# Last expert of a mixture-of-experts block: three whole-row loads and one in two column halves, with tokens added in PSUM

## The chip, the cores and the metric

The kernel runs on one core of a Trainium2 chip. Times are microseconds of device time of one execution. Three executions of the kernel before gave a median of 1518.48 us, from 1516.9 to 1519.0. The profile shown is of a further execution, which took 1518.31 us itself, with a span of 1516.6 us between its first and last recorded instruction.

## The reference, cut to what matters

Two transformer blocks on 256 tokens of width 1024. The second ends in a mixture of 16 experts; each expert takes the 32 tokens that score highest for it, and the rows that it gives are added to the tokens. A final RMS norm closes the program. What runs ahead (first block, mixers, cross attention) is left out here.

```python
def ec_moe(h, router_w, w_gu, w_down):
    ...
    gates, idx = lax.top_k(jnp.swapaxes(aff, 1, 2), cap)          # cap = 32
    def expert(args):
        xe, wgu, wd = args
        gu = jnp.einsum('bcd,df->bcf', xe, wgu)                   # 1024 -> 4096
        ga, up = jnp.split(gu, 2, axis=-1)
        return jnp.einsum('bcf,fd->bcd', jax.nn.silu(ga) * up, wd)  # 2048 -> 1024
    ...                                                           # gate, scatter-add

x = x + ec_moe(rmsnorm_2(x, norm_ffn_g), router_w, w_gu, w_down)
return rmsnorm_2(x, final_norm_g)        # x * rsqrt(mean(x*x) + eps) * g
```

All is float32. One expert has 16 MB of gate and up weights and 8 MB of down weights.

## The kernel before, in words

The last part of the program is `moe`. For each expert `e` it loads the gate and up weights (`w_gu`, four loads of 4 MB from expert 2 on, 32 KB in a row on each partition) and the down weights (`w_down`, four loads of 2 MB, 16 KB in a row on each partition). All loads are issued by SyncE (SP) into a ring of slots, and a load waits until TensorE has read what its slot held. TensorE multiplies the 32 tokens with the gate and up weights as they land (L1314), ScalarE and VectorE make `silu(gate) * up` (L1334, L1335), TensorE turns that round (L1338), ScalarE copies it out (`aT`, L1340), and the helper `down(j, raw, c0, n)` multiplies it with row block `j` of the down weights into the PSUM tile `y[c0]` (L1347). The four row blocks of one expert are called loads 0 to 3 below. The helper `scatter(c0, n, out, ...)` copies `y[c0]` to SBUF (`ys`, by ScalarE at L1357 or VectorE at L1359) and multiplies it with the gated one-hot matrix `ogT` (L1361), which adds the expert's rows to the tokens, one matrix product for each of the two token tiles `t`. Experts 0 to 14 add up in four PSUM banks `acc[2 * t + n]` (token tile `t`, column half `n`).

After expert 14 VectorE adds the four banks to the tokens `x` (L1374). Expert 15 goes another way. Its loads 0 and 1 are whole-row loads (L1395). Load 2 comes in two column halves. Load 3 comes in columns 0 to 511, 512 to 767, 768 to 895 and 896 to 1023 (all at L1401). For each of these four column pieces (`cuts`) the kernel finishes the products, scatters them to fresh PSUM tiles, adds them to `x` (L1410) and takes the sum of squares (L1411). Then `rstd` makes 1/sqrt with a bit trick and three Newton steps on VectorE (L171 to L181), two operations scale the halves of each token tile (L1417 on ScalarE, L1418 on VectorE), and two stores of 512 KB end the program (L1420).

`rstd_q`, used in the first block, makes 1/sqrt from ScalarE's square root, a reciprocal and one Newton step (L257 to L268). The order of instructions on each engine comes from a scheduler; the context manager `strict` (L102) makes PE, VectorE and ScalarE keep the written order inside it.

## Time and profile before

| | |
|---|---|
| three executions | 1516.9 to 1519.0 us, median 1518.48 |
| the profiled execution | 1518.31 us, of which span 1516.6 us |
| TensorE / VectorE / ScalarE busy | 77% / 28% / 23% of the span |
| bytes read from HBM | 500.79 MB |
| expert part | from about 640 us to the end |
| last expert's down loads | 8 MB, then the scatter, the norm and two stores |

TensorE is busy the most, but in the expert part most of its idle time is spent waiting for weights. The page's 40 slices show how much the DMA engines moved in each fortieth of the span. The timeline has one line for a run of equal instructions, with start and length, and in brackets how long the engine had been idle and what ended that.

### The profile page before, as it was taken

Reading aid. Unit: us, or ns where it says so; the run is one execution under the profiler, and the core shown is the slowest. Engines: PE = TensorE matmul, PEld = TensorE weight load, DVE = VectorE, ACT = ScalarE, POOL = GpSimd, SP = SyncE. Lnnn points to the kernel's source line nnn. Section 1 sums busy time; section 2 is a strip of 40 time slices with the busy share of each in tenths; the row PEclk is TensorE's granted clock in tenths of the full one; section 3 lists DMA queues with packets and bytes.
Section 4 is the critical chain, followed back from the end, with each engine's and each line's share of the span. In section 5 each row is a group of like instructions: output and inputs, shape, how many; then the busy total and the mean of one; then the engine's idle time right before and its main releaser. Section 6 shows DMA issues by size and latency. Waiting matters only on the chain.

```text
span 1516.6 us, 17752 instructions
## 1 busy us (share of the span) xinstructions
PE 1162.6 (77%) x7704; PEld 690.8 (46%) x7704; DVE 424.4 (28%) x801; ACT 355.5 (23%) x614; POOL 7.0 (0%) x19
## 2 busy tenths in 40 slices
PE   7999999999999999885665656665656656556665
PEld 5989989999988776321121111121111112111112
DVE  6744567445568864200000000000000000000002
ACT  6545546434456733000000000000000000000002
POOL 1000000000000000000000000000000000000000
PEclk9999999999999999997888877889888889888788
DMA  9754538555643279999999999999999999999996
GB/s 304 226 167 139 167 116 273 182 184 191 201 131 99 85 293 423 393 430 428 433 431 425 432 425 434 429 427 433 429 428 431 430 427 434 430 426 432 427 431 239
DMA packets 98189, 502.98 MB, mean 332 GB/s; under 512 B 8107, under 2 KB 62143, under 8 KB 80960
## 3 DMA queue, kind: packets, MB, share of 16 engines
q1 hardware_dynamic: 98112, 501.85, 82.6%
q8 instruction: 60, 0.98, 0.3%
q14 instruction: 17, 0.14, 0.0%
HBM read 500.79 MB, written 1.05 MB: 331 GB/s over the span
## 4 chain that ended last, share of the span: by engine, by line
PE 70%; another core or an unknown queue 16%; DMA 5%; DVE 3%; SPq 2%; ACT 2%; issue 1%; DVEq 0%; ACTq 0%
PE acc L127 21%; PE sm L1314 18%; PE sm L127 10%; PE sm L1347 9%; PE acc L1361 4%; DMA eraw<-in_expert_w_down_dram 2%; DMA eraw<-in_expert_w_gu_dram 2%; SPq L1401 2%; PE sm L1284 1%; PE acc L1171 1%; PE sm L1338 1%; DVE es L1335 1%; DVE ys L1359 1%; ACT aT L1340 1%
## 5 line engine op out<-in xcount | busy, mean ns | idle before, releaser
L1314 PE MATMUL sm<-eraw,xs 128*32 128x512 f32 x2048 | 319.0, 779 | 222.9 <-DMA eraw<-in_expert_w_gu_dram 222.9
L1314 PEld LDWEIGHTS sm<-eraw,xs 128*32 128x32 f32 x2048 | 77.0, 138 | 447.4 <-issue 230.8
L74 DVE TENSOR_TENSOR whl<-raw,whl 128x1024 fp32r<-128x1024 f32 x152 | 181.7, 1221 | 105.9 <-ACT whl L73 104.8
L1347 PE MATMUL sm<-eraw,aT 128*32 128x512 f32 (+2 forms) x1088 | 145.1, 669 | 66.2 <-DMA eraw<-in_expert_w_down_dram 54.5
L73 ACT ACTIVATE whl<-raw 128x1024 fp32r<-128x1024 f32 x152 | 154.0, 1052 | 78.0 <-issue 47.2
L1335 DVE SCALAR_TENSOR_TENSOR es<-sm,rsl,es 128x512 f32<-128x512 f32 x16 | 12.0, 751 | 439.5 <-PE sm L1314 436.6
L1334 ACT ACTIVATE es<-sm,rsl 128x512 f32<-128x512 f32 x16 | 11.0, 687 | 408.4 <-PE sm L1314 408.4
L1347 PEld LDWEIGHTS sm<-eraw,aT 128*32 128x32 f32 x1088 | 32.5, 120 | 161.5 <-DMA eraw<-in_expert_w_down_dram 89.6
L127 PE MATMUL acc<-xh,whl 128*128 128x256 f32 x704 | 96.2, 285 | 0.0
L127 PE MATMUL sm<-xh,whl 128*128 128x256 f32 x704 | 91.4, 283 | 0.0
L127 PEld LDWEIGHTS acc<-xh,whl 128*128 128x128 f32 x704 | 88.4, 189 | 1.1
L127 PEld LDWEIGHTS sm<-xh,whl 128*128 128x128 f32 x704 | 87.9, 189 | 0.6
L1361 PE MATMUL acc<-ys,ogT 128*128 128x512 f32 (+2 forms) x136 | 65.2, 603 | 15.2 <-DVE ys L1359 14.4
L1359 DVE COPY ys<-sm 128x512 f32<-128x512 f32 (+2 forms) x18 | 11.4, 631 | 196.9 <-PE acc L1361 196.9
L127 PE MATMUL acc<-whl,xh 128*128 128x512 f32 x240 | 65.9, 405 | 0.2
L1332 ACT ACTIVATE ogT<-sm 128x256 f32<-128x256 f32 x16 | 6.1, 383 | 220.6 <-PE sm L1330 220.6
L127 PE MATMUL acc<-whl,aH 128*128 128x512 f32 x176 | 55.9, 390 | 0.0
L1357 ACT ACTIVATE ys<-sm 128x512 f32<-128x512 f32 x16 | 9.6, 597 | 196.5 <-PE sm L1347 196.5
L1361 PEld LDWEIGHTS acc<-ys,ogT 128*128 128x128 f32 x136 | 23.2, 193 | 59.8 <-DVE ys L1359 27.7
L127 PE MATMUL acc<-xl,whl 128*128 128x256 f32 x352 | 50.1, 283 | 0.0
L127 PEld LDWEIGHTS acc<-whl,xh 128*128 128x128 f32 x240 | 44.6, 190 | 10.9 <-ACT xh L162 0.8
L127 PE MATMUL sm<-xl,whl 128*128 128x256 f32 x352 | 49.4, 283 | 0.0
(392 smaller groups left out, 1171.6 us busy)
## 6 DMA issues: line engine op xcount, KB each, us to landing
eraw<-in_expert_w_gu_dram SPq DMA_DIRECT2D x56, 4096.0 KB, 53.0
eraw<-in_expert_w_down_dram SPq DMA_DIRECT2D x62, 2048.0 KB, 55.2
raw<-in_w_in_dram SPq DMA_DIRECT2D x34, 1024.0 KB, 5.4
eraw<-in_expert_w_gu_dram SPq DMA_DIRECT2D x16, 2048.0 KB, 16.1
raw<-in_w_gate_dram SPq DMA_DIRECT2D x11, 1024.0 KB, 5.3
raw<-in_w_up_dram SPq DMA_DIRECT2D x11, 1024.0 KB, 5.6
raw<-in_w_down_dram SPq DMA_DIRECT2D x11, 1024.0 KB, 5.0
raw<-in_w_out_dram SPq DMA_DIRECT2D x8, 1024.0 KB, 5.1
```

Of the source, the lines that this page charges most:

```text
L73: nc.scalar.activation(H[:, k], raw[:, k], AF.Copy)
L74: self.at["L"] = nc.vector.tensor_tensor(L[:, k], raw[:, k], H[:, k].bitcast(F32), OP.subtract).ins
L127: nc.tensor.matmul(out, l[i], r[j], start=first and p == 0 and q == 0, stop=last and p == 2 and q == n - 1)
L1171: nc.tensor.matmul(acc[c], o[:, k, t * 128:(t + 1) * 128], w[c][:, k, :], start=k == 0, stop=k == 3)
L1284: nc.tensor.matmul(pg[kk][:, i * 128:(i + 1) * 128], x[:, t, feats(k)], OH[:, t, e:e + 4, :].rearrange("p e s -> p (e s)"), start=t == 0, ...
L1314: nc.tensor.matmul(dst[32 * j:32 * j + 32, :], xs[:, k, 32 * q:32 * q + 32], raw[:, o + 512 * j:o + 512 * j + 512], start=k == 0, stop=k = ...
L1335: nc.vector.scalar_tensor_tensor(s, U, rs, s, OP.mult, OP.mult)
L1338: nc.tensor.transpose(p[:, c * 128:(c + 1) * 128], s[:, c:512:4], self.ident)
L1347: nc.tensor.matmul(y[c0][32 * c:32 * c + 32, 0:n], aT[:, c, 32 * j:32 * j + 32], raw[:, o:o + n], start=j == 0, stop=j == 3, tile_position ...
L1359: nc.vector.tensor_copy(ys, y[c0][:, 0:n])
L1361: nc.tensor.matmul(out[t], ogT[:, t * 128:(t + 1) * 128], ys, start=first, stop=last)
L1401: nc.sync.dma_start(raws[j].rearrange("p (i n) -> p i n", i=4)[:, :, c0:c0 + m], rows(j)[:, :, c0:c0 + m])
```

## The change

- The last expert's loads 0, 1 and 2 are whole-row loads now, and load 3 comes in two column halves, each with rows of 2 KB.
- The tokens `x` are added in PSUM: after expert 3's scatter, four products of `x` with the identity matrix go into `acc`. The VectorE additions at L1374 and L1410 are gone, and the last expert scatters into `acc` as all others do.
- The squares and the product with the gain read `acc` directly. The last two lines of each token tile scale what is in `fo`.
- The second half's `ys` is copied by VectorE (256 columns) and ScalarE (256 columns).
- `strict` fixes the order from load 3 to the stores. `rstd_q` takes both token tiles and replaces `rstd`; a small square root behind the last `silu` has ScalarE load the square root's table there.

```diff
-    def rstd_q(self, ss):
+    def rstd_q(self, *sums):
...
+        for ss in sums:
+            q = self.small.tile([128, 8], F32, name="rstq", tag="rsq", bufs=4)
+            v, d, h, y, t = (q[:, i:i + 1] for i in range(5))
+            nc.vector.tensor_scalar(v, ss[:, 0:1], ss[:, 1:2], 1.0 / D, OP.add, OP.mult)
+            nc.scalar.activation(d, v, AF.Sqrt, bias=self.eps)
+            nc.vector.tensor_scalar(h, v, -0.5, -0.5 * EPS, OP.mult, OP.add)
+            qs.append((d, h, y, t))
+        for d, h, y, t in qs:
+            nc.vector.reciprocal(y, d)
+            nc.vector.tensor_scalar(t, y, y, h, OP.mult, OP.mult)
+            nc.vector.tensor_scalar(y, t, 1.5, y, OP.add, OP.mult)
+        return y if len(sums) == 1 else [q[2] for q in qs]
...
                     ys = ew.tile([128, n], F32, name="ys", tag="ys")
-                    if c0 == 0:
+                    if e == NE - 1 and c0:
+                        nc.vector.tensor_copy(ys[:, 0:256], y[c0][:, 0:256])
+                        nc.scalar.activation(ys[:, 256:512], y[c0][:, 256:512], AF.Copy)
+                    elif c0 == 0:
...
+                if e == 3:
+
+                    for t in range(2):
+                        for n in range(2):
+                            nc.tensor.matmul(acc[2 * t + n], self.ident, x[:, t, 512 * n:512 * n + 512],
+                                             start=False, stop=False)
+
...
-            raws, y[768], y[896] = {}, self.ps(), self.ps()
-            cuts = ((0, 512), (512, 256), (768, 128), (896, 128))
-            for i, (c0, n) in enumerate(cuts):
...
+            with self.queued([silu]):
+                nc.scalar.activation(fo[:, 0, 0:1], self.eps, AF.Sqrt)
+            raws = [slot() for _ in range(4)]
+            for j in range(3):
+                nc.sync.dma_start(raws[j], rows(j).rearrange("p i n -> p (i n)"))
+                for n in range(2):
+                    down(j, raws[j], 512 * n, 512)
+            for n in range(2):
+                c = slice(512 * n, 512 * n + 512)
+                nc.sync.dma_start(raws[3].rearrange("p (i n) -> p i n", i=4)[:, :, c], rows(3)[:, :, c])
+            ss = [self.small.tile([128, 16], F32, name="ss", tag="st1", bufs=4) for _ in range(2)]
+            with self.strict():
+                for n in range(2):
+                    c = slice(512 * n, 512 * n + 512)
+                    down(3, raws[3], 512 * n, 512)
+                    scatter(512 * n, 512, acc[n::2], False)
+                    for t in range(2):
+                        nc.scalar.activation(junk, acc[2 * t + n], AF.Square, accum_out=ss[t][:, n:n + 1])
+                        nc.vector.tensor_tensor(fo[:, t, c], acc[2 * t + n], g[:, c], OP.mult)
+                r = self.rstd_q(*ss)
                 for t in range(2):
...
+                    nc.scalar.activation(fo[:, t, 0:512], fo[:, t, 0:512], AF.Copy, scale=r[t])
+                    nc.vector.tensor_scalar(fo[:, t, 512:D], fo[:, t, 512:D], r[t], None, OP.mult)
```

The loads of the last expert, as they stand on SyncE in the kernel before (`raw` slots of SBUF are called `eraw`; a wait on DMAHW waits for an earlier load, a wait on PE, DVE or Activation for that engine):

```order
L1377 DMA eraw<-in_final_norm_g_dram 1x1024 [waits DMAHW5_49,DMAHW1_49,PE_49]
L1395 DMA eraw<-in_expert_w_down_dram 128x4096 [waits DMAHW2_49]
L1395 DMA eraw<-in_expert_w_down_dram 128x4096 [waits DMAHW3_49]
L1401 DMA eraw<-in_expert_w_down_dram 128x4x512 [waits DMAHW4_49]
L1401 DMA eraw<-in_expert_w_down_dram 128x4x512
L1401 DMA eraw<-in_expert_w_down_dram 128x4x512 [waits DMAHW6_49]
L1401 DMA eraw<-in_expert_w_down_dram 128x4x256 [waits DMAHW7_49]
L1401 DMA eraw<-in_expert_w_down_dram 128x4x128 [waits DMAHW0_49]
L1401 DMA eraw<-in_expert_w_down_dram 128x4x128 [waits DMAHW1_49]
```

The same place in the changed kernel:

```order
L1386 DMA eraw<-in_final_norm_g_dram 1x1024 [waits DMAHW5_49,DMAHW1_49,PE_49]
L1396 DMA eraw<-in_expert_w_down_dram 128x4096 [waits DMAHW2_49]
L1396 DMA eraw<-in_expert_w_down_dram 128x4096 [waits DMAHW3_49]
L1396 DMA eraw<-in_expert_w_down_dram 128x4096 [waits DMAHW4_49]
L1401 DMA eraw<-in_expert_w_down_dram 128x4x512
L1401 DMA eraw<-in_expert_w_down_dram 128x4x512 [waits DMAHW6_49]
```

Eight down loads have become five, and the first half of load 3 stands behind three whole loads, where it stood behind two whole loads and a half.

VectorE from the last expert's first scatter result to the start of 1/sqrt, in the kernel before:

```order
L1410 TENSOR_TENSOR x<-x,acc 128x512 [waits PE_49]
L1413 TENSOR_TENSOR eraw<-x,eraw 128x512 [waits DMAHW2_49,DMAHW5_49,DMAHW1_49,DMAHW6_49,DVE_49,Activation_49]
L1410 TENSOR_TENSOR x<-x,acc 128x512 [waits PE_49]
L1413 TENSOR_TENSOR eraw<-x,eraw 128x512 [waits DVE_49]
L1359 COPY ys<-sm 128x256 [waits PE_49,Activation_49]
L1410 TENSOR_TENSOR x<-x,acc 128x256 [waits PE_49] x2
L1359 COPY ys<-sm 128x128 [waits DVE_49]
L1410 TENSOR_TENSOR x<-x,acc 128x128 [waits PE_49] x2
L1359 COPY ys<-sm 128x128 [waits DVE_49]
L1410 TENSOR_TENSOR x<-x,acc 128x128 [waits PE_49] x2
L1414 TENSOR_REDUCE ss<-ss 128x2 [waits Activation_49]
```

VectorE at the same place in the changed kernel:

```order
L1410 TENSOR_TENSOR eraw<-acc,eraw 128x512 [waits DMAHW5_49,DMAHW2_49,DMAHW6_49,DMAHW1_49,Activation_49]
L1410 TENSOR_TENSOR eraw<-acc,eraw 128x512 [waits Activation_49]
L1361 COPY ys<-sm 128x256 [waits PE_49]
L1410 TENSOR_TENSOR eraw<-acc,eraw 128x512 [waits Activation_49] x2
L264 TENSOR_SCALAR rstq<-ss 128x1
L266 TENSOR_SCALAR rstq<-rstq 128x1 [waits DVE_49]
```

The additions to `x` are gone, each product with the gain waits for ScalarE, and the copy of `ys` stands behind both products of the first half.

ScalarE from the last `silu` to the square roots in the changed kernel:

```order
L1338 ACTIVATE es<-sm,rsl 128x512 [waits PE_49]
L1393 ACT_TABLE_LOAD [waits DMAHW5_49,DMAHW6_49,DMAHW2_49]
L1393 ACTIVATE eraw<-eps 128x1 [waits DMAHW1_49]
L1344 ACTIVATE aT<-sm 128x512 [waits PE_49,Activation_49]
L1390 ACTIVATE eraw<-sm 128x512 [waits PE_49] x2
L1364 ACTIVATE ys<-sm 128x512 [waits PE_49,Activation_49]
L1409 ACTIVATE eraw,ss<-acc 128x512 [waits PE_49]
L1409 ACTIVATE eraw,ss<-acc 128x512 [waits PE_49,Activation_49]
L1362 ACTIVATE ys<-sm 128x256 [waits DVE_49]
L1409 ACTIVATE eraw,ss<-acc 128x512 [waits PE_49]
L1409 ACTIVATE eraw,ss<-acc 128x512 [waits PE_49,Activation_49]
L265 ACTIVATE rstq<-rstq,eps 128x1 [waits DVE_49] x2
```

A table load and a small square root have come between `silu` and `aT`, and ScalarE's half of `ys` waits for VectorE's half. On TensorE the only rows that change ahead of the last expert are the four products with the identity: one stands between the two scatters of expert 3 and three behind the second. All else that differs is the products of the last expert's loads and scatters.

## Rows read from the trace of the kernel before

**Rows 1.** The page: GB/s moved in each of 40 equal slices of the span.

```profile
GB/s 304 226 167 139 167 116 273 182 184 191 201 131 99 85 293 423 393 430 428 433 431 425 432 425 434 429 427 433 429 428 431 430 427 434 430 426 432 427 431 239
```

**Rows 2.** Two SyncE lines: the second whole load, and load 3's first half: start, us.

```profile
1458.85 0.42 SPq L1395 DMA_DIRECT2D eraw<-in_expert_w_down_dram  x1
1459.96 2.11 SPq L1401 DMA_DIRECT2D eraw<-in_expert_w_down_dram  x1
```

**Rows 3.** The same two loads among DMA issues: size, us from issue to landing.

```profile
eraw<-in_expert_w_down_dram SPq DMA_DIRECT2D x1, 2048.0 KB, 33.1
eraw<-in_expert_w_down_dram SPq DMA_DIRECT2D x1, 1024.0 KB, 37.3
```

**Rows 4.** Timeline of expert 14's end: start, us, instructions, idle before and its releaser.

```profile
1438.38 3.25 PE L1347 MATMUL sm<-eraw,aT 128*32 128x512 f32 x16 [2.56 <-DMA eraw<-in_expert_w_down_dram]
1443.27 1.92 PE L1347 MATMUL sm<-eraw,aT 128*32 128x512 f32 x16 [1.64 <-DMA eraw<-in_expert_w_down_dram]
...
1447.96 1.98 PE L1361 MATMUL acc<-ys,ogT 128*128 128x512 f32 x4 [0.85 <-DVE ys L1359]
...
1449.99 0.69 DVE L1374 TENSOR_TENSOR x<-x,acc 128x512 f32<-128x512 f32 x1 [0.17 <-PE acc L1361]
```

**Rows 5.** Timeline of the last expert, from aT to the stores.

```profile
1489.76 0.60 ACT L1340 ACTIVATE aT<-sm 128x512 f32<-128x512 f32 x1 [1.88 <-PE sm L1338]
...
1497.30 1.06 PE L1347 MATMUL sm<-eraw,aT 128*32 128x512 f32 x8 [1.28 <-DMA eraw<-in_expert_w_down_dram]
1498.49 0.60 ACT L1357 ACTIVATE ys<-sm 128x512 f32<-128x512 f32 x1 [6.28 <-PE sm L1347]
...
1499.14 1.98 PE L1361 MATMUL acc<-ys,ogT 128*128 128x512 f32 x4 [0.78 <-ACT ys L1357]
...
1500.30 0.69 DVE L1410 TENSOR_TENSOR x<-x,acc 128x512 f32<-128x512 f32 x1 [11.44 <-PE acc L1361]
...
1501.06 1.73 PE L1347 MATMUL sm<-eraw,aT 128*32 128x256 f32 x40
...
1503.02 0.42 DVE L1359 COPY ys<-sm 128x256 f32<-128x256 f32 x1
...
1511.53 1.01 SPq L1420 DMA_DIRECT2D out_dram<-eraw  x2
```

**Rows 6.** Timeline where block one squares and scales a PSUM bank and calls rstd_q.

```profile
214.10 0.60 ACT L254 ACTIVATE pj<-acc 128x512 bf16<-128x512 f32 x1 [7.49 <-PE acc L127]
...
214.82 1.45 DVE L286 TENSOR_TENSOR pn<-acc,gain 128x512 f32<-128x512 f32 x2 [6.30 <-ACT pj L254]
...
215.57 1.28 ACT L263 ACT_TABLE_LOAD   x1
...
220.31 0.21 DVE L262 TENSOR_SCALAR rstq<-ss 128x1 f32<-128x1 f32 x1 [0.94 <-ACT pj L254]
...
220.88 0.17 DVE L265 RECIPROCAL rstq<-rstq 128x1 f32<-128x1 f32 x1 [0.17 <-ACT rstq L263]
...
221.64 1.42 DVE L216 SCALAR_TENSOR_TENSOR hn<-x,rstq,gain 128x512 f32<-128x512 f32 x2
```

**Rows 7.** One group of instructions: busy us, mean ns of one, idle before.

```profile
L1332 ACT ACTIVATE ogT<-sm 128x256 f32<-128x256 f32 x16 | 6.1, 383 | 220.6 <-PE sm L1330 220.6
```

**Rows 8.** Windows: us, PE, PEld, DVE, ACT, POOL busy; granted PE clock, DMA share, GB/s.

```profile
1476.40:1479.70 3.30, 1.36 (x15) 0.14 (x5) 0.00 (x0) 0.00 (x0) 0.00 (x0) 1.00 0.97 417
1479.80:1483.20 3.40, 1.06 (x8) 0.40 (x12) 0.00 (x0) 0.00 (x0) 0.00 (x0) 0.50 0.99 424
...
1493.40:1496.90 3.50, 2.62 (x44) 0.96 (x32) 0.00 (x0) 0.00 (x0) 0.00 (x0) 1.00 0.90 312
1496.90:1500.30 3.40, 2.22 (x11) 0.83 (x12) 0.00 (x0) 0.60 (x1) 0.00 (x0) 1.00 0.66 224
1500.30:1503.70 3.40, 2.69 (x43) 1.32 (x42) 3.00 (x5) 1.45 (x4) 0.00 (x0) 1.00 0.21 64
```

**Rows 9.** Timeline of TensorE at the first weights after expert 3.

```profile
805.39 1.07 PE L1314 MATMUL sm<-eraw,xs 128*32 128x512 f32 x8 [3.13 <-DMA eraw<-in_expert_w_gu_dram]
```

58 lines of the change are left out of this document (7 added, 51 removed).

## The prediction

> **What bounds the kernel now.** I read the page's slices first. From the 18th of 40 slices on, the DMA engines move about 430 GB/s without a break [rows 1]: the expert part is bound by the weights that stream in, and what engines do beside that stream costs nothing until the stream ends. So the change can matter in two places only: where it might disturb the stream (expert 3), and in the stretch from the last weights to the last store. The timeline of that stretch is the second view [rows 5]: TensorE waits for the first half of load 3 (1497.30), the scatter starts at 1499.14, and the pair of stores is issued from 1511.53 to 1512.54. I rebuild this stretch on the clock of the profiled execution and compare the end of the two store issues. All else, 1518.31 us less the stretch, I leave as it is.
>
> **Loads.** A load's landing is its issue plus the time to landing. The second whole load (load 1) landed at 1458.85 + 33.1 = 1491.95, the first half of load 3 at 1459.96 + 37.3 = 1497.26 [rows 2, 3]. Between the two lie 5.31 us and 2 MB in rows of 2 KB (half of load 2, half of load 3), so 2.65 us for 1 MB. Whole-row loads of 2 MB follow each other by 1443.27 - 1438.38 = 4.89 us, read from two products that each waited for its load [rows 4], 2.45 us for 1 MB. In the change load 1 lands as before, then comes load 2 whole, then load 3's halves: 1491.95 + 4.89 = 1496.84, + 2.65 = 1499.49 for the first half, + 2.65 = 1502.14 for the second. The first half lands 2.2 us later than before, since 1 MB more stands ahead of it. That is the price of the change; what it removes behind that point is the gain.
>
> The Trainium skill, page "DMA: Bandwidth & Descriptors", section "Specifications", gives 512 B as the least transfer for full rate, so by that rule longer rows bring nothing. The trace speaks against it (2.65 against 2.45 us for 1 MB); by the rule the first half would land at 1499.9 and the whole sum come out 0.4 us later.
>
> **First half.** Load 2 needs 16 product rows, 1.92 us at full clock [rows 4], so it is done at 1498.8, before load 3's first half. From the landing of the first half, before: products at 1497.30, `ys` at 1498.49, scatter at 1499.14, which is 1.88 us behind the landing (1497.26); first scatter result read at 1500.30, 1.16 us on [rows 5]. The second result of a scatter is read 1449.99 - 1447.96 = 2.03 us behind its start [rows 4]. TensorE is free for the next product 1501.06 - 1499.14 = 1.92 us behind it [rows 5]. In the change: scatter at 1501.37, results at 1502.53 and 1503.40, TensorE free at 1503.29. The fixed order puts the second half's products behind this scatter, so the second half, landed at 1502.14, waits 1.15 us for TensorE. Its products give `y` 1.19 us later (1497.30 to 1498.49), at 1504.48.
>
> **VectorE and ScalarE.** The order shows that each product with the gain waits for the square of the same bank on ScalarE. Block one has the same pair: the square starts at 214.10, the product at 214.82, so 0.72 us behind it, and a product takes 1.45/2 = 0.73 us [rows 6]. The squares start at 1502.53 and 1503.40, the products at 1503.25 and 1504.12, the second ends at 1504.85. Behind it in VectorE's queue stands its half of `ys`: it could start at 1504.48 and starts at 1504.85, takes 0.42 us [rows 5], and only then ScalarE's half starts, 0.38 us by a copy of the same shape [rows 7]. Twice 0.05 us go for handing over (1499.09 to 1499.14 in rows 5). The second scatter starts at 1505.75. One VectorE copy of 512 columns would have been 0.69 us; the split takes 0.85 us. Then 2.03 us to the second result (1507.78), 0.72 us to its product (1508.50), 0.73 us for that: 1509.23.
>
> **1/sqrt, scaling, stores.** One `rstd_q` takes 221.64 - 220.31 = 1.33 us to the first use: 0.57 us to the reciprocal, 0.76 us from there [rows 6]. Here two run in one queue. The lower bound is 1.33 us for both, the upper 2.66 us one behind the other. Both starts go first (about 0.75 us), then the two ends, of which the second takes about 0.6 us in the shadow of none: 2.1 us, in the middle, since the queue is in order and its steps depend on one another. ScalarE's second scaling takes 0.71 us more (1.42/2 in rows 6, VectorE's likewise). So the second store is ready at 1509.23 + 2.1 + 0.71 = 1512.04 and, with 0.06 us to its issue, goes at 1512.1. Before, the second issue began at 1512.54 - 0.35 = 1512.19, with 0.35 us for one of the two [rows 5]. **The sum:** 1512.1 against 1512.19, -0.1 us, within what the working can tell. Bounds of the unknown part: -0.8 us (1/sqrt at 1.33 us) to +0.6 us (2.66 us).
>
> **What costs nothing, and its cover.** The table load takes 1.28 us [rows 6] and a square root at most 0.57 us more (one lies between 220.31 and 220.88 in rows 6), between `silu` and `aT`; ScalarE was idle for 1.88 us there [rows 5]. If the cover is too short by some tenths, load 0's products come later, but TensorE then still has to wait about 2 us for load 2 (below), which takes that up. The four products with the identity are 4 x 0.99 = 4.0 us of TensorE at most (a scatter of two takes 1.98 us, rows 4). TensorE waits 3.13 us for the first weights after expert 3 [rows 9], so these weights are begun at most 0.9 us late, and the loads that wait for a slot are queued far ahead (33 us from issue to landing in rows 3). The VectorE additions behind expert 14 lay beside the weight stream and give back nothing. On SyncE five loads are issued where eight were; nothing is queued behind them but the stores.
>
> **The rivals.**
>
> *TensorE falls to half clock (slower).* From 1493.4 to 1503.7 the granted clock was full [rows 8]. In the gate and up loads, where TensorE waits for every load, it went from 1.00 in the row of 1476.40 to 0.50 in that of 1479.80, which is 1.2 instead of 2.4 GHz [rows 8]. The 16 products behind a wait of 2.56 us took 3.25 us, those behind a wait of 1.64 us took 1.92 us [rows 4]. In the change the products of loads 0 and 1, 3.8 us together and begun behind `aT` at about 1491, are over at about 1495; then TensorE waits for load 2 until 1496.9, a wait of 1.9 us that the kernel before does not have and that lies between those two rows. If load 2 alone is run at half clock, its 16 rows take 3.8 us, until 1500.7 at the latest, where load 3's first half could have started at 1499.5: up to +1.2 us. If half clock holds on, every step doubles: +0.9 us for the half's products, +1.7 us for the scatter that TensorE has to finish first, +0.9 and +1.7 us for the second half, in all about 6 us, 1524 us. The point from which it decides is half clock through the first scatter (1.2 + 0.9 + 1.7 = 3.8 us, 1522). Against that: full clock did come back between the 0.50 of 1479.80 and the 1.00 of 1493.40, while TensorE had the last gate and up products to do, and the waits of the kernel before in this stretch (1.28 us in rows 5) did not lower it. One stretch: 0.16. Through the first scatter: 0.05. The Trainium skill, page "TensorE: Matmul & The Clock Gate", section "Loop structure matters more than you think", says the same of loops that wait for a DMA between matrix products: TensorE goes cold. By that rule the change, which leaves TensorE a longer wait for load 2, would pay at least the one stretch.
>
> *The falling rate at the end is a fault of short rows (faster).* From 1493.4 to 1503.7 the stream falls to 312, 224 and 64 GB/s [rows 8]. These rows moved 312 x 3.5 + 224 x 3.4 + 64 x 3.4 = 2070 KB. At 410 GB/s they would take 5.05 us and not 9. If whole rows kept the rate, the second half would land at 1498.5 and the first 2.5 us ahead of it at 1496.0, 3.5 us earlier than in my sum: 1514.7 us. Against it: the landings themselves come at 2.65 us for 1 MB up to 1497.26, hardly slower than in the stream. Chance 0.06, half of that beyond 3 us.
>
> *Reads side by side.* If square and product, and the two halves of `ys`, ran at once, the sum would be 0.4 us (the wait of the copy), 0.4 us (one half of `ys`) and 0.7 us (the last product) shorter: 1516.8 us. The waits in the order exclude it as built, so 0.08, for a shorter end in whatever way.
>
> *Row length brings nothing:* load 2 takes 2 x 2.65 instead of 4.89 us, the first half lands 0.4 us later and all behind it with it: 1518.6 us, 0.07. *Expert 3's products do hold up the stream,* all 4 us: 1522.2 us, 0.02.
>
> **How the numbers follow.** About 0.2%, or 3 us, is what a measurement of this kernel can tell from no change; faster means below 1515.4, slower above 1521.5. My own case, 0.56: 1518.31 - 0.1 = 1518.2 us, within 0.2%, which stands 0.3 us under the median of the three executions. The forecast is no change. Slower by over 0.2%: half clock through the scatter and expert 3, 0.07. Faster by over 0.2%: half of the second rival, 0.03. The rest, 0.90, is within. Range: low end 1516.8 (reads side by side, also the lowest of the three executions), high end 1520.0 (one stretch at half clock, 1519.4, and 0.5 us for the spread of executions). Outside lie the 0.10 just named and the edges of the others.
>
> **What would show it.** Right: the first half of load 3 landing near 1499.5 and the scatter 1.9 us behind; TensorE going from the first scatter to the second half's products without a wait for a DMA; VectorE's `ys` behind two products; stores at about the same distance from load 1's landing, 20 us. Wrong: a granted clock under 1 between 1486 and 1510, a TensorE wait for the second half of load 3 (the stream then ends later than I say), an idle TensorE before `aT`'s products longer than before, or any expert from 4 to 14 that takes longer than its neighbours before.

## The result: 8.7 us faster, and not where the change was made

The changed kernel takes 1510.05 us (median of four, 1509.06 to 1510.26) against 1518.73 us for the kernel before (median of four): 0.9944 of its time, 95% interval 0.9927 to 0.9961. I had forecast no change, 1518.2 us. The profiled execution took 1510.26 us itself.

The span is the first line; the second shows the 40 slices of GB/s of the changed kernel, which answer [rows 1].

```profile
core 0: 1508.5 us, clock 0.904
```

```profile
GB/s 304 228 168 147 161 146 262 187 188 196 206 101 127 98 314 425 393 429 427 432 429 429 429 430 429 431 425 434 429 426 434 430 425 435 430 424 433 429 428 239
```

The stream of expert weights runs at the same 430 GB/s and ends in the same kind of slice. So the next view is SyncE's issues, which mark the same place of the program in both kernels. Three issues of the kernel before (start, us it took, line, tile, count): a gate load early in the first block's feed-forward part, one in its middle, and the first expert loads, which begin well ahead of the 640 us that the table of the kernel before gives for the expert part.

```profile
208.59 0.37 SPq L62 DMA_DIRECT2D raw<-in_w_gate_dram  x1
...
305.04 0.37 SPq L62 DMA_DIRECT2D raw<-in_w_gate_dram  x1
...
549.17 28.58 SPq L1230 DMA_DIRECT2D eraw<-in_expert_w_gu_dram  x8
```

The same three of the changed kernel:

```profile
204.40 0.37 SPq L62 DMA_DIRECT2D raw<-in_w_gate_dram  x1
...
299.13 0.37 SPq L62 DMA_DIRECT2D raw<-in_w_gate_dram  x1
...
540.91 28.69 SPq L1234 DMA_DIRECT2D eraw<-in_expert_w_gu_dram  x8
```

It is 4.19 us ahead at the first, 5.91 at the second, 8.26 at the third. From the first expert load to the end of the span both take the same: 1516.6 - 549.17 = 967.4 us before, 1508.5 - 540.91 = 967.6 us after. **The whole gain lies ahead of the experts, in code that the change does not touch**, and grows bit by bit, not at one place. What grows it is TensorE's commonest product, line 127. The kernel splits activations and weights each into a rounded value and the remainder: `xh` and `xl` are the two parts of the activations, and `whl` holds both parts of a weight tile. Groups of instructions of the kernel before (count | busy us, mean ns of one | idle before):

```profile
L127 PE MATMUL acc<-xh,whl 128*128 128x256 f32 x704 | 96.2, 285 | 0.0
L127 PE MATMUL sm<-xh,whl 128*128 128x256 f32 x704 | 91.4, 283 | 0.0
```

and of the changed kernel:

```profile
L127 PE MATMUL acc<-xh,whl 128*128 128x256 f32 x704 | 93.1, 280 | 0.0
L127 PE MATMUL sm<-xh,whl 128*128 128x256 f32 x704 | 89.7, 280 | 0.0
```

3.1 and 1.7 us less for these two groups. Durations overlap here, so the spacing is better: the mean distance between the starts of neighbouring products of this form (activations `xh` or `xl` against weights `whl`), worked out from the starts of about 1890 pairs in each trace, is 119.3 ns before and 115.6 ns after. There are 2112 such products, 2112 x 3.7 ns = 7.8 us, nearly all of the 8.26.

The tail itself did what the prediction said. Its timeline in the changed kernel, which answers [rows 5]:

```profile
1488.95 1.92 PE L1351 MATMUL sm<-eraw,aT 128*32 128x512 f32 x16 [2.21 <-DMA eraw<-in_expert_w_down_dram]
...
1491.62 1.07 PE L1351 MATMUL sm<-eraw,aT 128*32 128x512 f32 x8 [0.74 <-DMA eraw<-in_expert_w_down_dram]
...
1493.46 1.98 PE L1368 MATMUL acc<-ys,ogT 128*128 128x512 f32 x4 [0.78 <-ACT ys L1364]
...
1495.37 1.06 PE L1351 MATMUL sm<-eraw,aT 128*32 128x512 f32 x8
...
1496.87 0.41 DVE L1361 COPY ys<-sm 128x256 f32<-128x256 f32 x1
1497.32 0.38 ACT L1362 ACTIVATE ys<-sm 128x256 f32<-128x256 f32 x1 [1.09 <-DVE ys L1361]
...
1497.76 1.98 PE L1368 MATMUL acc<-ys,ogT 128*128 128x512 f32 x4 [1.32 <-ACT ys L1362]
...
1500.56 0.69 DVE L1410 TENSOR_TENSOR eraw<-acc,eraw 128x512 f32<-128x512 f32 x1 [0.23 <-ACT eraw L1409]
...
1503.58 0.84 SPq L1415 DMA_DIRECT2D out_dram<-eraw  x2
...
1504.06 0.37 SPq L1415 DMA_DIRECT2D out_dram<-eraw  x1
```

The last line is the second of the two stores by itself.

### The profile page after: what moved, and what is told of

Its sections match the earlier page's. It is cut to its first block, busy times and chain, and to the rows that moved or that the text cites. A ratio compares the mean times of both kernels' runs of the same rounds, so it can differ in the third digit from the quotient of the medians.

```text
span 1508.5 us, 17599 instructions
## 1 busy us (share of the span) xinstructions
PE 1158.1 (77%) x7640; PEld 681.4 (45%) x7640; DVE 418.5 (28%) x786; ACT 356.7 (24%) x611; POOL 7.0 (0%) x19
## 4 chain that ended last, share of the span: by engine, by line
PE 69%; another core or an unknown queue 16%; DMA 7%; DVE 4%; ACT 2%; issue 1%; SPq 0%; DVEq 0%; ACTq 0%
PE acc L127 20%; PE sm L1318 18%; PE sm L127 9%; PE sm L1351 9%; DMA eraw<-in_expert_w_down_dram 5%; PE acc L1368 4%; DMA eraw<-in_expert_w_gu_dram 2%; PE sm L1288 1%; PE acc L1175 1%; PE sm L1342 1%; DVE es L1339 1%; ACT aT L1344 1%; DVE ys L1366 1%; DMA x<-in_x_dram 0%
## 5 line engine op out<-in xcount | busy, mean ns | idle before, releaser
L1351 PE MATMUL sm<-eraw,aT 128*32 128x512 f32 x1024 | 144.7, 699 | 68.7 <-DMA eraw<-in_expert_w_down_dram 56.9
L127 PE MATMUL acc<-xh,whl 128*128 128x256 f32 x704 | 93.1, 280 | 0.0
L1368 PE MATMUL acc<-ys,ogT 128*128 128x512 f32 x128 | 64.7, 628 | 14.0 <-DVE ys L1366 11.9
L1366 DVE COPY ys<-sm 128x512 f32<-128x512 f32 x15 | 10.4, 692 | 212.5 <-PE acc L1368 212.5
```

The lines of the kernel that those rows point to most:

```text
L127: nc.tensor.matmul(out, l[i], r[j], start=first and p == 0 and q == 0, stop=last and p == 2 and q == n - 1)
L1351: nc.tensor.matmul(y[c0][32 * c:32 * c + 32, 0:n], aT[:, c, 32 * j:32 * j + 32], raw[:, o:o + n], start=j == 0, stop=j == 3, tile_position ...
L1366: nc.vector.tensor_copy(ys, y[c0][:, 0:n])
L1368: nc.tensor.matmul(out[t], ogT[:, t * 128:(t + 1) * 128], ys, start=first, stop=e == NE - 1)
```

## Why addresses were suspected

The change deletes the call of `rstd` at the end of the program. That was the only user of one small tile: 32 bytes per partition, two slots, the last 64 bytes of the pool `small`. Every tile allocated behind that pool therefore starts 64 bytes lower; by the two programs' lists of tiles, `whl` moved from 21344 to 21280 (bytes within a partition), while `xh` and `xl`, allocated from the other end of the memory, stay at 212960 and 221152. Nothing in the diff says so. Call the **distance** of a product the start of `whl` less the start of `xh`, counted within 256 bytes: 128 before, 64 after. (256 is a choice for counting; how far it is borne out stands at e4.)

The theories: A, addresses are the cause, later sharpened to D, the distance of a product's two operands; B, the code (fewer instructions, another place of the program). In the table the first expert load is that of the one profiled execution, and each ratio is to executions of the kernel before that were measured beside that version.

| run | distance | first expert load at us | median us | ratio to before, 95% interval |
|---|---|---|---|---|
| before | 128 | 549.17 | 1518.73 | |
| changed | 64 | 540.91 | 1510.05 | 0.9944 (0.9927 to 0.9961) |
| e1 changed + 64 bytes | 128 | 548.73 | 1518.07 | 0.9998 (0.9989 to 1.0008) |
| e2 before, 64 bytes lower | 64 | 541.16 | 1510.94 | 0.9952 (0.9937 to 0.9967) |
| e3 changed + 128 bytes | 192 | 544.90 | 1514.38 | 0.9973 (0.9962 to 0.9984) |
| e4 only `memH` lower | 64 | 541.55 | 1510.17 | 0.9947 (0.9932 to 0.9962) |
| e5 `xh`, `xl` lower | 128 | 549.84 | 1518.75 | 1.0002 (0.9992 to 1.0012) |
| e6 changed + 192 bytes | 0 | 548.61 | 1518.26 | 0.9998 (0.9988 to 1.0008) |
| e7 changed + 32 bytes | 96 | 547.83 | 1515.69 | 0.9987 (0.9977 to 0.9996) |
| e9 changed, 32 bytes lower | 32 | 547.66 | 1513.08 | 0.9963 (0.9948 to 0.9977) |
| e13 changed, run again | 64 | 540.59 | 1510.58 | 0.9947 (0.9933 to 0.9961) |
| e14 `whl` and `xh` 32 lower | 64 | 541.78 | 1506.89 | 0.9925 (0.9913 to 0.9938) |

## Experiments on the cause

**e1: the changed kernel with the 64 bytes put back.** An unused tile, no instruction. (The statement stands at the end of a line that is there already; so do those of e4, e5, e14 and e16.)

```diff
+            self.small.tile([128, 16], F32, name="pad", tag="pad", bufs=1)
```

> The changed kernel with one unused tile of 64 bytes per partition added to the pool of small tiles, at its end, so that every tile behind that pool (the split weights whl first of all) lies where it lay in the kernel before; the instructions are those of the changed kernel, one for one. Theory A (addresses): the stretch ahead of the experts ran 8.4 us shorter after the change because those tiles lie 64 bytes lower; then it is lost again, the 128x256 products of the line for whl take 283 to 285 ns instead of 278 to 280, and what stays is the tail's own gain of 0.2 us: 1518.3 us, ratio to the kernel before 0.9995 to 1.0005. Theory B (code: fewer or shorter instructions, another position of the program, anything but addresses): 1510.1 us as the changed kernel, ratio 0.9944. Theory C (the chip or the day): no fixed forecast, between the two.

1518.07 us: the gain is gone. B falls.

**e2: the kernel before without the 64 bytes.** Its last small tile goes into slots of another tile; instructions are the same, one for one.

```diff
-        q = self.small.tile([128, 4, n], F32, name="rstd", tag=tag + str(n), bufs=4 if n == 1 else 2)
+        q = self.small.tile([128, 4, n], F32, name="rstd", tag="rsq" if n == 2 else tag + str(n), bufs=2 if n > 2 else 4)
```

> The kernel before with its instructions one for one, but its last small tile (the 1/sqrt at the end) put into slots that an earlier tile of the same size has, so that every tile behind the pool of small tiles lies 64 bytes lower, as in the changed kernel. Theory A (addresses): the 8.2 us come without the change's edits, 1518.7 less 8.4 is 1510.3 us, ratio 0.9942 to 0.9950. Theory B (code): 1518.7 us, ratio 1.000.

1510.94 us: nearly all of the gain, without one line of the change. e1 and e2 together show that the 8 us belong to the addresses. The edits themselves are worth too little to be told from nothing: 1518.07 us for e1 against 1518.55 for the kernel before beside it, with an interval that holds 1.

**e3 and e4: which address.** e3 uses 128 unused bytes instead of 64. e4 was to move `xh` and `xl`, but the pad fell below them in their pool; only `memH`, the memory tokens of the cross attention, moved (188384 to 188320).

```diff
-        self.xt = self.open("xt", 1, self.xtp, "right")
+        self.xt = self.open("xt", 1, self.xtp, "right"); self.xt.tile([128, 16], F32, name="pad", tag="pad")
```

> The changed kernel with an unused tile of 128 bytes in place of the 64: tiles behind the small pool lie 128 bytes higher than in the changed kernel and 64 higher than in the kernel before. Theory A1 (only the address within 128 bytes matters, 32 is fast and 96 slow): 1510.1 us. Theory A2 (the distance matters, whatever lies higher is slower, or a longer period): 1518 us or another time. Theory B: 1510.1 us.

> The changed kernel with the tiles of whl left where it has them, and 64 unused bytes in the pool at the other end of the memory, so that the stationary activations xh and xl stand at the same place within 128 bytes as in the kernel before, less 64 (32 instead of 96). Theory A3 (what matters is how whl and xh lie to each other within 128 bytes: both at 96 in the kernel before, 32 against 96 after the change): both are at 32 again, so the gain goes and the time is 1518 us. Theory A1 (whl's own place) : 1510.1 us, no change to the changed kernel. Theory B: 1510.1 us.

e3: 1514.38 us, between the two kernels, so the place of `whl` within 128 bytes is not enough (A1 falls). e4 left the time alone, 1510.17 us, and so says nothing of A3 for `xh`; but its one moved tile is a small experiment of its own. Two groups of line 127 in the changed kernel (count: ns min/median/max, first and last start), then in e4:

```profile
L127 PE MATMUL acc<-xl,whl x352: 276/276/366, 40.0 to 461.1; 128*128 128x256 f32 x176
...
L127 PE MATMUL sm<-memH,whl x64: 276/276/374, 221.6 to 233.5; 128*128 128x256 f32 x64
```

```profile
L127 PE MATMUL acc<-xl,whl x352: 276/276/366, 39.9 to 461.9; 128*128 128x256 f32 x176
...
L127 PE MATMUL sm<-memH,whl x64: 274/281/364, 221.5 to 233.6; 128*128 128x256 f32 x64
```

Only the products with `memH`, whose distance to `whl` went from 64 to 128, are longer (276 to 281 ns); those with `xl` in the same run are not. Their spacing goes from 117.0 to 121.2 ns, the 121.2 of the kernel before. `memH` lies 24576 bytes (96 times 256) below `xh` and follows the same rule, which bears out counting within 256 bytes; whether a shorter or a longer period would do as well was not tried.

**e5: `xh` and `xl` really moved, `whl` not.**

```diff
-        xT, factor, scale, trans = self.norm_T(self.x, "mix_pre_g")
+        xT, factor, scale, trans = self.norm_T(self.x, "mix_pre_g"); self.xt.tile([128, 16], F32, name="pad", tag="pad")
```

> The changed kernel with the tiles of whl left where they are and the activations xh and xl put 64 bytes lower (212896 in place of 212960; in the run before this one called e4_xh64 the 64 bytes landed below them, and only memH moved, so that run asked nothing of xh). Counted within 256 bytes, whl stands behind xh by 64 in the changed kernel, by 128 in the kernel before, by 192 with the pad of 128. Theory D (the distance between a product's two operands counts): it is 128 now, as in the kernel before, so the gain of 8 us goes: 1518 us, and the spacing of the 128x256 products is 119 ns. Theory W (whl's own address counts): whl has not moved, 1510.1 us, spacing 115.5 ns.

1518.75 us. `whl` lies where the changed kernel has it and the gain is gone all the same: the distance decides, not the place (D). The group of 352 products in the kernel before, in e5 and in e2:

```profile
L127 PE MATMUL acc<-xl,whl x352: 274/282/368, 40.3 to 469.2; 128*128 128x256 f32 x176
```

```profile
L127 PE MATMUL acc<-xl,whl x352: 274/282/368, 41.0 to 469.8; 128*128 128x256 f32 x176
```

```profile
L127 PE MATMUL acc<-xl,whl x352: 276/276/367, 40.7 to 461.3; 128*128 128x256 f32 x176
```

**e6, e7, e9: other distances.** 192 and 32 unused bytes in e1's place; for e9 two unused slots of a small tile are given up as well (`bufs=4` to `bufs=2` for the tile `bn`) and 96 unused bytes put in.

> The changed kernel with 192 unused bytes at the end of the small pool: whl stands at the same place within 256 bytes as xh (distance 0; 64 after the change, 128 before it, 192 with the pad of 128). Theory D with a cost that falls as the distance leaves 128 on either side (119.3 ns at 128, 117.3 at 192, 115.5 at 64): 113 to 116 ns at 0 and 1506 to 1511 us. Theory D with a cost for equal places, which would be the plainest collision: above 119 ns and over 1518 us. No theory that gives every 64 bytes the same: 1510 or 1518.

> The changed kernel with 32 unused bytes: the distance between whl and xh is 96 within 256. Theory D with a cost that goes gradually: half way between 64 (115.5 ns, 1510.1 us) and 128 (119.3 ns, 1518.3 us), so 117.4 ns and 1514 us. Theory D in steps of 64 bytes: 1510 us or 1518 us.

> The changed kernel with two unused slots of one small tile given up and 96 unused bytes added, so that whl stands 32 bytes lower and its distance behind xh is 32 within 256. So far: 0 gave 119.8 ns and 1518.3 us, 64 gave 115.5 and 1510.1, 96 gave 118.3 and 1515.7, 128 gave 119.3 and 1518.5, 192 gave 117.3 and 1514.4. Theory D with the same cost on both sides of a full meeting (0 or 128): 32 costs as 96, 118.3 ns and 1515.7 us. If only 64 bytes of lag help because the order in time counts, 32 lies between 0 and 64: 117 to 118 ns and 1513 to 1516 us. If 64 is not the best place: under 115 ns and under 1509 us.

Mean spacings, worked out as above: 119.9 ns at distance 0, 118.2 at 32, 115.6 at 64, 118.3 at 96, 119.3 at 128, 117.3 at 192. The first expert load follows them to within 2 us (table). The largest miss is e6, 0.56 us earlier than before at a dearer spacing. There the products the other way round help, 360 of 128x512 with `whl` stationary and `xh` or `xl` moving: their mean spacing is 232.5 ns before, 229.8 in the changed kernel and 227.8 in e6, and 360 x 4.7 ns = 1.7 us. Of the expectations e6's dearer case held (0 costs as much as 128), and so did e9's first one in its spacing (32 costs as 96); e7 lies between 64 and 128, but nearer to 128 than half way. For e9 the spacing did not give the whole time: its first expert load is 1.51 us earlier than before and its time 5.7 us less. That opened a second question (e14, below).

**e13: one program, two spacings.** The changed kernel unaltered, run again.

> The changed kernel, nothing altered, in the same call, as the base for e12 and to see whether one and the same program changes between the two spacings that its 128x256 products show (113 and 118 ns, each for a whole stretch). If the spacing of a stretch is settled by the program and its addresses, the trace repeats the one on record stretch for stretch and the times lie within 0.6 us of 1510.05. If it is settled by how a stretch happens to begin, some stretches change sides: a stretch of 250 products is worth 1.2 us, and single times lie between 1507 and 1513 us, as those of e10 did.

1510.58 us, single times 1508.96 to 1511.81. At distance 64 the products show two spacings, 113.3 and 117.8 ns, each for a whole stretch. A stretch of the changed kernel's timeline (start, us, engine, count), 8 products each from 121.89 and the next from 122.80, so 0.91 / 8 = 114 ns:

```profile
121.89 1.07 PE L127 MATMUL acc<-xl,whl 128*128 128x256 f32 x8
122.80 1.41 PE L127 MATMUL acc<-xh,whl 128*128 128x256 f32 x11
```

The same stretch in e13, 0.95 / 8 = 119 ns:

```profile
121.94 1.11 PE L127 MATMUL acc<-xl,whl 128*128 128x256 f32 x8
122.89 1.34 PE L127 MATMUL acc<-xh,whl 128*128 128x256 f32 x10
```

(The lines are rounded to 10 ns.) So some stretches change sides between executions of one program. Others do not: the products into `sm` from about 262 to 400 us are at 117.8 ns in both. At distance 128 (before) no stretch is at 113:

```profile
189.01 2.08 PE L127 MATMUL acc<-xh,whl 128*128 128x256 f32 x16
190.93 1.12 PE L127 MATMUL acc<-xl,whl 128*128 128x256 f32 x8
```

1.92 / 16 = 120 ns. What settles a stretch's spacing stays open; that a stretch holds it once begun was seen, not why.

**e14 and e15: the slots' own addresses.** `whl` shares its slots with a third of the expert loads' bytes. In e9 those slots begin at multiples of 256 bytes (21248); in e7 at a multiple of 64 (21312); in all others at neither. e14 lowers `whl` and `xh` together by 32 bytes: distance 64 as in the changed kernel, slots at 21248. e15 does this to the kernel of e12 (below).

```diff
-                st = self.small.tile([128, 16], F32, name="bn", tag="st2", bufs=4)
+                st = self.small.tile([128, 16], F32, name="bn", tag="st2", bufs=2)
+            self.small.tile([128, 24], F32, name="pad", tag="pad", bufs=1)
+        self.xt.tile([128, 8], F32, name="pad", tag="pad")
```

> The changed kernel with whl (and the expert loads' tiles that share its slots) and also xh and xl 32 bytes lower: the distance stays 64 within 256, but the slots now begin at multiples of 64 bytes, as in the two kernels at distances 96 and 32. Theory D alone (distance): first expert load issued at 541 us as in the changed kernel and 1510.3 us. Theory E (the expert stream is faster into slots at multiples of 64): the kernel at distance 32 began its experts 1.5 us earlier than the kernel before and ended 4.4 us of span earlier, so some 3 us came behind that point; then 1507.3 us here, with the first expert load again at 541 us. Rival to E: that stream scatters by 2 to 3 us between executions anyway, 1510.3 us.

> The same shift by 32 bytes on the kernel of e12 (last products interleaved, the second copy in its own slot), which took 1508.98 us. Theory D alone: 1509.0 us. Theory E (3 us from slots at multiples of 64): 1506 us.

1506.89 us (1505.60 to 1508.79) against e13's 1510.58 (1508.96 to 1511.81), and 1505.02 against e12's 1508.98. The two of a pair were not measured side by side; by their ratios to the kernel before (0.9925 against 0.9947, 0.9917 against 0.9934) the gains are 3.3 and 2.6 us. The first expert load comes at 541.78, as at distance 64, so the gain has to lie behind it. From the first expert load to the end of the span the profiled executions take 966.6 to 968.4 us in ten traces without such slots (before, changed, e1 to e7, e13), but 965.3 in e14 and 964.5 in e9, and 960.9 in e15 against e12's 965.4. The steady part of the stream, 740 to 1465 us, in the changed kernel, in e14 and in e16 (us, busy time of the engines, granted clock, DMA share, GB/s last):

```profile
740.00:1465.00 725.00, 447.67 (x2850) 128.71 (x2846) 28.61 (x55) 27.55 (x49) 0.00 (x0) 0.83 1.00 429
```

```profile
740.00:1465.00 725.00, 459.10 (x2858) 130.89 (x2862) 28.62 (x55) 27.62 (x49) 0.00 (x0) 0.81 1.00 431
```

```profile
740.00:1465.00 725.00, 463.92 (x2866) 131.95 (x2858) 29.30 (x56) 27.55 (x49) 0.00 (x0) 0.82 1.01 432
```

The same row reads 431 in e9 and e15, 430 in e7 and in the kernel before, 429 in e5, e6, e12 and e13. To a tenth, worked out from the transfers of each trace in this window: 429.4 in ten traces and 429.7 in four (before, e1, e3, e7) of kernels without such slots, 431.1 to 431.2 in e9, e14 and e15, 431.9 in e16 and e17. The step from 429.4 is 0.41%, and 0.41% of the some 950 us between the first expert load (541) and the last down load (landed by 1495) is 3.9 us, where the ratios show 3.3 and 2.6 and the stretches 1.3 (e14 against e13) to 4.4 us (e15 against e12). So theory E (the place of a slot counts for the stream) has the rate and the stretch behind the first expert load on its side. The expectation spoke of multiples of 64; e7, whose slots begin at one, has neither, so that it is 256 that fits. (e9, e14 and e15 share the edit to `bn` as well; it lies in the first block, far ahead of this window, and from e14 to e16 the rate rose again by a shift alone.) The Trainium skill, page "DMA: Bandwidth & Descriptors", section "How a descriptor splits into AXI transactions", says that a descriptor (one piece of a transfer) that does not start at a multiple of 256 bytes has its first transaction begin at the boundary below its start, so that unused bytes are moved too. It tells this of reading, and here it is the written side that moved; it would go with these numbers, though no run here shows the transactions.

**e16 and e17: all slots at multiples of 256.** 224 unused bytes above the remaining slots, on e14 and on e15.

```diff
-            est = ExitStack()
+            est = ExitStack(); self.open("epad", 1, es, "right").tile([128, 56], F32, name="pad", tag="pad")
```

> The kernel of e14 with the other expert slots moved too (224 unused bytes above them): all slots now begin at multiples of 256 bytes; in e14 only the four that share their place with whl did, and they take a third of the experts' bytes, in rows of 16 KB. e14 took 1506.89 us, 3.2 to 3.7 us less than the changed kernel. Theory E (a slot at a multiple of 256 is filled faster): the other two thirds of the bytes gain as well, by the byte 7 us, by the row (their rows are 32 KB, so as many rows) 3.5 us: 1500 to 1503.4 us. Rival (scatter between calls, or an effect of the stream's place that has nothing to do with the slots): 1506.9 us.

> The same on the kernel of e15 (tail interleaved), which took 1505.02 us. Theory E: 1498 to 1501.5 us. Rival: 1505.0 us.

1514.91 and 1512.26 us, 8 and 7 us slower: a miss. The rate did go up once more (432 above, and 432 in e17), but with the pad the first expert loads waited longer for a product of the cross attention (line 1163), perhaps because a slot now overlaps memory that it still uses; that reason is argued, not shown. SyncE's waits between 541 and 690 us (who was waited for: us, times, longest), in e14 and then in e16:

```profile
SPq L1234 <- PE po L1163: 13.2, 1, 13.2
```

```profile
SPq L1234 <- PE sm L1318: 27.6, 8, 11.4
SPq L1234 <- DMA eraw<-in_expert_w_down_dram: 24.0, 4, 15.6
SPq L1234 <- PE po L1163: 22.7, 1, 22.7
```

One wait of 13.2 us became 22.7 us, and what the stream does not move then it never makes up. From 541 to 580 us, in e14 and in e16:

```profile
541.00:580.00 39.00, 38.02 (x178) 27.52 (x177) 21.04 (x56) 16.09 (x40) 0.00 (x0) 1.00 0.94 384
```

```profile
541.00:580.00 39.00, 38.03 (x177) 27.41 (x176) 21.05 (x56) 16.05 (x40) 0.00 (x0) 1.00 0.73 297
```

87 GB/s less for 39 us is 3.4 MB, or 7.9 us of the stream. Theory E is supported by the rate and not by these two times.

## Experiments on the tail

**e8: no early table load.** The small square root behind the last `silu` is left out.

```diff
-            with self.queued([silu]):
-                nc.scalar.activation(fo[:, 0, 0:1], self.eps, AF.Sqrt)
```

> The changed kernel without the early square root after the last silu, so that the function table for the square root is loaded at the end, where the kernel before did without it. By the prediction's step the load took 1.28 us and was hidden in ScalarE's idle 1.88 us; here nothing hides it, it stands between the last sum of squares and the first square root: the way from the last half's product to the first store grows by 1.28 us, and the time by as much, 1511.3 us. If the load runs while VectorE still makes its first two small steps, 0.3 to 0.5 us of it stay hidden: 1510.9 us.

1509.11 us in its one execution. From the second half's products to the end of the store issues: 9.05 us in the changed kernel (1495.37 to 1504.42), 9.43 us here (1493.86 to 1503.29). Only 0.38 us of the 1.28 show in this pair of traces:

```profile
1499.02 1.28 ACT L265 ACT_TABLE_LOAD   x1
...
1499.65 0.20 DVE L264 TENSOR_SCALAR rstq<-ss 128x1 f32<-128x1 f32 x1
```

The load begins when ScalarE is free, before the first square root's input exists, and runs beside VectorE's last product. My expectation had at most 0.5 us of it hidden.

**e11: the last load whole.**

```diff
-            for n in range(2):
-                c = slice(512 * n, 512 * n + 512)
-                nc.sync.dma_start(raws[3].rearrange("p (i n) -> p i n", i=4)[:, :, c], rows(3)[:, :, c])
+            nc.sync.dma_start(raws[3], rows(3).rearrange("p i n -> p (i n)"))
```

> The changed kernel with its last load whole, in place of two column halves. By the prediction's loads a whole one lands 4.89 us behind the third, about when the second half landed (0.4 us earlier), and the first half's work can no longer begin 2.65 us behind the third. Since TensorE was not free for the second half until 1.15 us after it landed, the end moves by less than the 2.24 us that the first half waits: the whole stretch behind the landing of the first half moves by 2.2 us if TensorE's order is the limit throughout (1512.3 us), and by 1.1 us if the two halves' products then run together (1511.2 us). Rival (rows of 2 KB cost what rows of 16 KB save): the whole load lands over 1 us earlier than the second half and the end moves by under 1 us.

1513.69 us in its one execution. From load 2's products to the end of the store issues it takes 19.99 us (1488.02 to 1508.01) against 15.47 (1488.95 to 1504.42): 4.5 us more, where I had expected 1.1 to 2.2. Windows over the products of the half, the scatter and the next products (PE busy first, granted clock third from the end):

```profile
1492.90:1494.00 1.10, 1.07 (x8) 0.16 (x8) 0.00 (x0) 0.00 (x0) 0.00 (x0) 0.98 0.00 0
1494.70:1498.50 3.80, 3.74 (x8) 1.21 (x9) 0.69 (x1) 0.69 (x3) 0.00 (x0) 0.50 0.00 0
1498.50:1500.40 1.90, 1.90 (x9) 0.17 (x8) 0.69 (x1) 0.69 (x2) 0.00 (x0) 0.50 0.00 0
```

The granted clock is 0.50, 1.2 GHz, through the scatter, after TensorE had waited 2.19 us for load 2, worked for 1.92, and waited 2.97 us for the whole load. In the changed kernel the waits there are 2.21 and 0.74 us and the clock is 1.00. This is the first rival of the prediction, seen in a neighbour: 2.2 us because the work starts later, 1.8 us in the first scatter and 0.5 us in the next products. So in these two traces the two halves are worth 4.5 us, more than their earlier start. The Trainium skill, page "TensorE: Matmul & The Clock Gate", section "Loop structure matters more than you think", says that long waits for a DMA between products leave TensorE cold; e11 agrees. In the changed kernel, with its waits of 2.21 and 0.74 us, TensorE kept its clock.

**e10 and e12: another order at the end.** The second half's products go between the first half's two products into `acc`; the last quarter is scaled straight out of PSUM.

```diff
...
+                down(3, raws[3], 0, 512)
+                nc.scalar.activation(ys[0], y[0], AF.Copy)
+                put(ys[0], 0, 0)
+                down(3, raws[3], 512, 512)
+                put(ys[0], 0, 1)
+                square(0, 0)
+                nc.scalar.activation(ys[1], y[512], AF.Copy)
...
+                nc.vector.scalar_tensor_tensor(fo[:, 1, R], acc[3], r[1], g[:, R], OP.mult, OP.mult)
```

> The changed kernel, its addresses kept, with TensorE's last steps in another order: of the first half's two products into the sums only the one for tokens 0 to 127 stands ahead of the second half's down products, the other behind them, so that ScalarE's copy of the second half (now whole, 0.60 us) runs while TensorE is busy. And the last quarter is scaled out of PSUM in one step after 1/sqrt, so that nothing stands between the last sum of squares and 1/sqrt on VectorE. By the rows of the changed kernel: the second half's products would begin 0.95 us earlier (1494.42 for 1495.37), its first product into the sums 1.25 us earlier (1496.5 for 1497.76), and 1/sqrt begins right behind the last sum instead of 0.6 us later; from the first half's landing to the last store's issue about 1.8 us less, 1508.3 us. Rival: the copies out of PSUM queue behind squares on ScalarE as much as they gain: 1510 us.

> The kernel of e10 with the second half's copy in a slot of its own. In e10 both halves' copies had one slot, so ScalarE's second copy waited for the last of TensorE's products out of the first (copy at 1499.18, while its own products had ended by 1498.1), and from the first half's landing to the last store's issue only 0.92 us of the forecast 1.8 went. With the slot of its own the copy starts at the end of the second down products and the first product into the sums about 1 us earlier than in e10: 1.9 us less than the changed kernel from landing to last store, 1508.1 us where the changed kernel takes 1510.05. Rival: ScalarE is then the limit (four squares, one copy and two scalings queue on it) and only 0.3 to 0.5 us come on top of the 0.92.

e10 took 1511.59 us, but its four times spread from 1507.78 to 1512.73, so I read its trace: from the first half's products to the end of the store issues 11.88 us (1494.06 to 1505.94) against 12.80 (1491.62 to 1504.42), 0.92 less and not 1.8. The second copy waited for TensorE's products out of the first, since both had one slot:

```profile
1499.18 0.60 ACT L1422 ACTIVATE ys<-sm 128x512 f32<-128x512 f32 x1 [1.42 <-PE acc L1407]
```

With a slot of its own (e12: `ys = [ew.tile([128, 512], F32, name="ys", tag=tag) for tag in ("ys", "es")]`) it waits for its own products alone:

```profile
1496.32 0.60 ACT L1422 ACTIVATE ys<-sm 128x512 f32<-128x512 f32 x1 [0.34 <-PE sm L1351]
```

10.87 us (1492.29 to 1503.16), 1.93 less than the changed kernel, as expected, and 1508.98 us (1507.26 to 1509.43) against e13's 1510.58 beside it. With e14's addresses (e15) it is the fastest version: 1505.02 us, 0.9917 of the kernel before (0.9904 to 0.9931), faster than both kernels.

## Why the prediction was wrong

- **"All else, 1518.31 us less the stretch, I leave as it is": the step that failed.** It held for the instructions but not for the addresses. The deleted tile moved `whl` by 64 bytes, and all that runs ahead of the experts took 8.26 us less (e1, e2, e5). My figure for the term was 0, and no rival or bound covered it: all my rivals lay in the last 20 us or at expert 3. With the 64 bytes put back (e1) the changed kernel takes 1518.07 us, where I had 1518.2. The list of tiles of the two programs would have shown the shift; its price no row of the trace before shows.
- **Loads: right.** Load 2's products to the first half's are 1491.62 - 1488.95 = 2.67 us; I had 2.65 from [rows 2, 3].
- **First half: right.** Half to scatter 1.84 us (I had 1.88 behind the landing), TensorE free 1.91 us later (1.92), and the second half's products wait for no DMA, as said.
- **VectorE and ScalarE: right.** The two copies run one behind the other, 0.41 and 0.38 us; from scatter to scatter 4.30 us, I had 4.38; the last product begins 2.80 us behind the second scatter, I had 2.75.
- **1/sqrt and stores: right within 0.1 us.** From the second scatter to the second store's issue 6.30 us (1497.76 to 1504.06), I had 6.35. The middle of my bounds held.
- **Covers: right.** The first expert load to the end of the span is 967.4 us before and 967.6 after, so expert 3's four products cost nothing that can be read. TensorE's wait for the first weights behind them shrank from 3.13 us [rows 9] to 0.56, and those weights were begun as soon as they landed. The table load stood in ScalarE's idle time; in e8 it costs 0.38 us at the end, not 1.28.

```profile
797.05 3.64 PE L1318 MATMUL sm<-eraw,xs 128*32 128x512 f32 x32 [0.56 <-DMA eraw<-in_expert_w_gu_dram]
```

- **Rivals.** Half clock did not come in the changed kernel; e11 shows it behind a longer wait, 2.97 us. "A fault of short rows" can't be judged by the changed kernel alone, whose last 2 MB still come in rows of 2 KB. It falls with e11, where all rows are whole: the rate falls at the end all the same, and the last load lands 4.89 us behind the one before it (1488.02 to 1492.91), the pace of [rows 4]. Windows of e11:

```profile
1486.00:1489.00 3.00, 0.98 (x12) 0.39 (x16) 0.00 (x0) 0.00 (x0) 0.00 (x0) 1.00 0.56 229
1489.00:1492.40 3.40, 0.94 (x12) 0.03 (x4) 0.00 (x0) 0.00 (x0) 0.00 (x0) 1.00 0.39 164
```

"Row length brings nothing" falls too: load 2 landed 4.96 us behind load 1 (1483.98 to 1488.94) with whole rows, against 2 x 2.65 in rows of 2 KB.

- **What would show it.** I named stores 20 us behind load 1 and a full clock; both came out (20.1 us behind load 1's landing; 1.00 from load 0's products on), and the time was still 8 us off, since these checks, too, looked at the tail alone.

## What to carry to other kernels

A change that adds or drops a tile moves every tile behind it: compare the two programs' addresses before taking the rest of the kernel as it was, and when a time moves, first find out where along the program the two traces part. Treat operand distances and slot starts as something to tune by unused bytes, one shift at a time, and look for the new waits that a shift makes (e16). Two pieces of a last load can be worth more than the earlier start, if the wait for one large piece costs the clock (e11).

## What the runs showed of the hardware

- The spacing of 128x256 float32r products depends on how their stationary and moving operands lie to each other: 115.6 to 116.3 ns at distance 64 (twelve traces), 119.2 to 119.4 at 128, 119.9 at 0. Moving either operand alone changes it (e1, e5), moving both does not (e14). With the roles changed, `whl` stationary, products of 128x512 are closest at distance 0 (227.8 ns against 232.5 at 128). Why is open. The Trainium skill, page "SBUF — State Buffer", section "A bandwidth-pool intuition that's wrong (but worth ruling out)", gives the loading of weights a second, independent read port. If the two reads never met, their distance should not matter; e1 and e5 show that it does, and the measurement decides.
- At one distance, 64, stretches run at 113 or at 118 ns and hold it; some of them change sides between executions (e13). Open.
- The expert stream moved 429 to 430 GB/s with the slots' old starts, 431 with a third of the bytes in slots at multiples of 256 bytes (e9, e14, e15), 432 with all (e16, e17). That the place of the slots counts is borne out by these runs; the mechanism is not shown.
- In the tail the granted clock fell to 0.50 after waits of 2.19 and 2.97 us with 1.92 us of products between them (e11), and stayed at 1.00 after waits of 2.21 and 0.74 us (changed kernel).
